# Start addresses of weight tiles, transposed activations and the SwiGLU product in a two-layer hybrid trunk

## The chip, the cores and the metric

The kernel runs on one core of a Trainium2 chip. The metric is the device time of one execution in microseconds (us). Before the change it is 2417.23 us, the median of three runs (2416.89 to 2418.15).

## What is computed

Two layers of a streaming-encoder trunk on one sequence of 256 rows by 2048 columns, in float32. Each layer projects the rows, runs three groups of heads, mixes them, and applies a SwiGLU feed-forward part; a layer norm follows each half.

```python
for li in range(DEPTH):                                   # DEPTH = 2
    proj = x @ w_in[li]                                   # 2048 -> 6920 columns
    qa, ka, va, qb, kb, vb, qc, kc, vc, oc, ic, fc = jnp.split(proj, SPLIT_POINTS, axis=-1)
    ya = diff_attention(qa, ka, va, lam[li], subln_a[li], li)
    yb = chunk_band_attention(qb, kb, vb, rel_bias[li])
    yc = mlstm(qc, kc, vc, oc, ic, fc, conv_w[li], norm_c[li])
    mix = jnp.concatenate([ya, yb, yc], axis=-1) @ w_out[li]          # 2048 -> 2048
    x = layer_norm(DEEPNORM_ALPHA * x + mix, ln1_g[li], ln1_b[li])
    ffn = (jax.nn.silu(x @ w_gate[li]) * (x @ w_up[li])) @ w_down[li] # 2048 -> 5632 -> 2048
    x = layer_norm(DEEPNORM_ALPHA * x + ffn, ln2_g[li], ln2_b[li])
```

## The kernel before

Almost all of the work is the products with the weights. `run_groups` works through them as a list of groups. In a layer there are seven input groups, `in.0` to `in.6` (`w_in`, 1024 columns each, the last 768), two groups for `w_out`, and then, for each half of the 5632 feed-forward columns, six groups for gate and up (1024, 1024 and 768 columns, first gate and then up: `ff.half.width.gate_or_up`) and two groups for `w_down` (`dn.half.block`). A group is a loop over `k`, steps of 128 rows of the weight (16 steps, in a `dn` group 22), and over `t`, the two halves of the sequence. Each float32 operand is held as two parts, a rounded one (`hi`) and the rest (`lo`), both of type float32r, and each product is made from three: `xh` by `whi`, `xh` by `wlo`, `xl` by `whi`. In TensorE's terms the piece of the transposed x (128 by 128) is the stationary operand, which a weight-load instruction brings into the array ahead of its matmul, and the weight row block (128 by 512, 384 or 256) is the moving one. A step of a group with two blocks is therefore six matmuls with six weight loads, all issued at L272:

```python
for i, (lt, wt) in enumerate(((xh, hi), (xh, lo), (xl, hi))):
    for b in bs:
        o, w = g["blocks"][b]
        nc.tensor.matmul(banks[t, b][:, 0:w], lt, wt[:, o:o + w], ...)
```

The order of the program is the order in which this Python code emits it; nothing is rescheduled. `convert` (L215) makes `whi` by a ScalarE cast (L224) and `wlo` by a VectorE subtraction (L225) from `raw`, which SyncE loads two steps at a time. `whi` and `wlo` have six buffers each, `raw` three. The stationary pieces come from two places. For the input, output, gate and up groups they lie in `xth` and `xtl`, made by `new_xt` (L288): a tile holds four `k` steps of 256 columns, there are four buffers ("slots") of each name, and a group goes through all four, four `k` steps in each. In the `dn` groups they lie in `gth` and `gtl` (L1031), one tile each that holds all 22 steps of the SwiGLU product. In the two names a piece is 512 bytes in each partition, and a piece starts a multiple of 512 bytes into its tile.

Between the products, `Tasks.tick` lets smaller tasks emit their instructions: attention heads, transposes, layer norm. `t_g` (L1085) transposes the SwiGLU product with 32x32 VectorE transposes (L408) and splits it into `gth` (ScalarE, L285) and `gtl` (VectorE, L286). The results of a group leave PSUM by ScalarE or VectorE (L428, L1037, L1041, L315); five PSUM banks serve the products, so a group's first matmul can wait for such an evacuation.

Of the kernel before, what the change touches and what calls it, by code (L numbers as in the profile page):

```python
# [10 lines left out]
F32 = mybir.dt.float32  # L11
F32R = mybir.dt.float32r
# [5 lines left out]
P = 128  # L18
SEQ = 256
# [14 lines left out]
KH = HALF_FF // P  # L34
# [11 lines left out]
FAR_AHEAD = 4  # L46
EVAC_ACT = (0, 1)
LAST_SKEW = 6
WARM = 9
MM_BUFS = 5  # L50
AUX_BUFS = 3
# [21 lines left out]


class Tasks:
    """Work that fills in between the weight products, a stage at a time.

    Units (attention heads) hold several buffers, so only a few of them run at once."""

    def __init__(self):  # L80
        self.q = []
# [46 lines left out]


def bcast(ap, n, offset, pattern):  # L130
    """A DRAM view read alike by n partitions."""
    return bass.AP(tensor=ap.tensor, offset=ap.offset + offset, ap=[[0, n]] + pattern)


class Trunk:
# [14 lines left out]
        self.flags = set()  # L150
        self.cms = {}

    # ---------------------------------------------------------------- set-up
    def setup(self):
        nc = self.nc
        c = self.const.tile([P, CONST_W], F32, name="cst_sb")
        self.cst_sb = c
        nc.scalar.dma_start(out=c[:, 0:P], in_=self.cst[:, 0:P])
        self.ident = c[:, 0:P]
        self.tri = c[:, P:2 * P]  # L160
        self.ones = c[:, 2 * P:3 * P]
        self.cmask = c[:, 3 * P:4 * P]
        o = 4 * P
        self.abias = c[:, o:o + A_HEADS * SEQ].rearrange("p (h k) -> p h k", h=A_HEADS)
        self.xs = [self.res.tile([P, D], F32, name=f"x{t}") for t in range(NT)]
        self.load_x(nc.sync, 0, 0)
        warm = self.const.tile([P, 512], BF16, name="warm")
        nc.vector.memset(warm, 0.0)
        wps = self.aux()
        for i in range(WARM):  # L170
            nc.tensor.matmul(wps, warm[:, 0:P], warm, start=True, stop=True)
        self.mhalf = self.const.tile([P, 2], F32, name="mhalf")
        nc.vector.memset(self.mhalf, -0.5)

    def load_x(self, eng, t, c):
# [20 lines left out]
    def aux(self):  # L196
        return self.psum.tile([P, 512], F32, name="aux", tag="aux", bufs=AUX_BUFS)

    # ------------------------------------------------------------- weight flow
    def load_pair(self, p):  # L200
        if p >= len(self.pairs):
            return
# [27 lines left out]
            self.load_pair(j // 2 + RAW_BUFS)  # L230

    def run_groups(self, groups):
        """Products x @ W over all groups; W streams through, split into two exact parts."""
        nc = self.nc
        self.steps, self.pairs, self.raws, self.whl = [], [], {}, {}
        for g in groups:
            g["base"] = len(self.steps)
            for k in range(g["nk"]):
                self.steps.append((g, k))
                if k % 2 == 0:  # L240
                    self.pairs.append(g["src"](k))
        for p in range(RAW_BUFS):
            self.load_pair(p)
            for c in {1: (1,), 2: (2, 3)}.get(p, ()):
                for t in range(NT):
                    self.load_x(nc.sync, t, c)
        done = 0
        for g in groups:
            nk, nb, si, so = g["nk"], len(g["blocks"]), g.get("skew_in", 1), g.get("skew_out", 1)
            allb = tuple(range(nb))  # L250
            order = [(k, t, allb) for t in range(NT) for k in range(si)]
            order += [(k, t, allb) for k in range(si, nk - so) for t in range(NT)]
            order += [(k, t, (b,)) for t in range(NT) for b in allb for k in range(nk - so, nk)]
            banks = {}
            g["start"]()
            for (k, t, bs) in order:
                j = g["base"] + k
                if (k, t, bs[-1]) == (nk - 1, NT - 1, nb - 1) and "mid" in g:
                    g["mid"]()
                xh, xl = g["lhs"](k, t)  # L260
                ahead = AHEAD if k >= nk - so or k < si else FAR_AHEAD
                while done < min(j + ahead + 1, len(self.steps)):
                    self.convert(done)
                    done += 1
                hi, lo = self.whl[j]
                for b in bs:
                    if (t, b) not in banks:
                        banks[t, b] = self.psum.tile([P, 512], F32, name="mm", tag="mm", bufs=MM_BUFS)
# [3 lines that stand above are left out]
                        nc.tensor.matmul(banks[t, b][:, 0:w], lt, wt[:, o:o + w],  # L272
                                         start=(k == 0 and i == 0), stop=(k == nk - 1 and i == 2))
                g["progress"] = k + 1
                if k == nk - 1:
                    for b in bs:
                        g["evac"](t, b, banks[t, b])
                if "after" in g and bs[-1] == nb - 1:
                    g["after"](k, t)
                if bs[-1] == nb - 1:  # L280
                    self.tasks.tick(g.get("budget", BUDGET) * g["width"] / 1024)

    # -------------------------------------------------------------- transposes
    def split(self, ps, hi, lo):
        self.nc.scalar.copy(out=hi, in_=ps)  # L285
        self.nc.vector.tensor_tensor(out=lo, in0=ps, in1=hi.bitcast(F32), op=ALU.subtract)  # L286

    def new_xt(self):  # L288
        return [self.xtp.tile([P, 4, SEQ], F32R, name=n, tag=n, bufs=4) for n in ("xth", "xtl")]

    def tr_block(self, srcs, dst, slot0, t):
        """Transpose [128 x 128] pieces into consecutive slots of a split block."""
        ps = self.aux()
        for i, s in enumerate(srcs):
            self.nc.tensor.transpose(out=ps[:, i * P:(i + 1) * P], in_=s, identity=self.ident)  # L295
        n = len(srcs)
        v = ps[:, 0:n * P].rearrange("p (k q) -> p k q", q=P)
        hi = dst[0][:, slot0:slot0 + n, t * P:(t + 1) * P]
        lo = dst[1][:, slot0:slot0 + n, t * P:(t + 1) * P]
        self.split(v, hi, lo)  # L300

    # ------------------------------------------------------------- layer norm
    def ln_load(self, g, b, l):
        nc = self.nc
        lg = self.lnpool.tile([P, D], F32, name="lng", tag="lng")
# [34 lines left out]
        nc.vector.scalar_tensor_tensor(out=z, in0=z, scalar=rs, in1=lb[:, s], op0=ALU.mult, op1=ALU.add)  # L340

    def xt_hooks(self, mvrs):
        """The transposed x by pieces: the first ones at once, the later ones while the products run."""
        xt = self.xt = [None] * 4
        applied, done = set(), set()
        piece = lambda k: next(i for i, (a, b) in enumerate(PIECES) if a <= k < b)
# [36 lines left out]
                    need(1, i)  # L383
        return dict(lhs=lhs, after=after, apply=apply, need=need)

    # ------------------------------------------------------------------ layer
    def attn_consts(self, l):
        nc, ap = self.nc, self.apool
        self.wg = self.const.tile([P, KD, 8], F32, name="wg", tag="wg")
# [12 lines left out]
        return self.apool.tile([P, 4, SEQ + 3], F32, name="qk", tag="qk", bufs=5)  # L402

    def dve_tr(self, out, in_, n):
        """Transpose n [128 x 128] tiles of in_ [P, n, 128] into out [P, n, 128] in four stages."""
        for i in range(4):
            for j in range(4):
                self.nc.vector.transpose(out=out[32 * j:32 * j + 32, 0:n, 32 * i:32 * i + 32],  # L408
                                         in_=in_[32 * i:32 * i + 32, 0:n, 32 * j:32 * j + 32])
            yield 1, 0.05 + 0.19 * n  # L410
# [7 lines left out]
        (self.nc.scalar.copy if t in EVAC_ACT else self.nc.vector.tensor_copy)(out=out, in_=in_)  # L418

    def evac_qk(self, t, bank, dst, scaled, scale, flag):  # L420
        """The first `scaled` of four tiles are queries and take the scale of the scores."""
        nc = self.nc
        stg = self.stg_tile()
        n = scaled * P
# [7 lines left out]
        while not all(f in self.flags for f in fl):  # L432
            yield 1, 0.0

    # -- C ---------------------------------------------------------------------
    def t_conv(self, l, blk):
        nc = self.nc
        yield from self.wait_flags("conv", (("cqk", blk), 0), (("cqk", blk), 1))
# [17 lines left out]
    def t_gates(self, l):  # L456
# [9 lines left out]
        for k in range(KD):  # L466
# [3 lines left out]
                                 stop=(k == KD - 1 and i == 2))  # L470
            if k % 8 == 7:
                yield 1, 0.0
        gT = ap.tile([8, SEQ], F32, name="gT")
        nc.scalar.copy(out=gT, in_=ps[0:8, 0:SEQ])
        yield 1, 0.3
        ps = self.aux()
# [111 lines left out]
        yield 1, 0.6  # L588

    def rms(self, ss, n, r):  # L590
        """r * (ss / n + eps) ** -0.5, all [P, k]."""
        nc = self.nc
        k = ss.shape[-1]
        ve = self.small.tile([P, 2], F32, name="rve")
# [29 lines left out]
            self.nc.gpsimd.tensor_tensor(out=y, in0=y, in1=self.nrm, op=ALU.mult)  # L624
        yield 1, 0.0

    # -- B ---------------------------------------------------------------------
    def t_bscore(self, h0, t):
        nc, ap = self.nc, self.bpool
        nb = t + 1  # L630
# [61 lines left out]
            self.flags.add(("B", h0, u))  # L692
        yield 1, 0.6

    # -- A ---------------------------------------------------------------------
    def t_aprep(self, l):
        nc, ap = self.nc, self.apool
        lam_init = 0.8 - 0.6 * math.exp(-0.3 * l)
# [72 lines left out]
        self.flags.add(("A", h, t))  # L771
        yield 1, 0.2

    # -- mix -------------------------------------------------------------------
    def mix_block(self, b):
        if self.mixt[b] is None:
            self.mixt[b] = self.new_xt()
        return self.mixt[b]

    def mix_ready(self, k, t):  # L780
        """Whether the k-th block of 128 columns of the mix (C, A, B) is in place."""
        return (("mix", k // 4, t) if k < 10 else ("B", (k - 10) // 2 * 2, t)) in self.flags

    def t_mix(self, b, t, last_in):
# [13 lines left out]
        self.flags.add(("mix", b, t))  # L798
        yield 1, 0.6

    # -- the groups of a layer ---------------------------------------------------
    def rows(self, w, l, r0, c0, width):
        return w[l, r0:r0 + 2 * P, c0:c0 + width].rearrange("(k p) n -> p k n", p=P)

# [209 lines left out]
    def ffn_groups(self, l):  # L1014
# [3 lines left out]
        for hf in range(2):  # L1018
            c = 0
            for wi, w in enumerate(widths):  # L1020
# [4 lines left out]
                for gu in range(2):  # L1025
# [2 lines left out]

                    def start(hf=hf, wi=wi, gu=gu):
                        if wi == 0 and gu == 0:  # L1030
                            self.gt = [self.gpool.tile([P, KH, SEQ], F32R, name=n, tag=n) for n in ("gth", "gtl")]  # L1031

                    def evac(t, b, bank, gu=gu, bw=bw, kt0=kt0, hf=hf):
                        nc = self.nc
# [96 lines left out]
```

## Time and profile before

| | before |
|---|---|
| median of 3 runs | 2417.23 us |
| profiled execution, span from first to last instruction | 2413.9 us |
| PE (TensorE matmul) busy | 2351.6 us, 97% of the span |
| PEld (weight loads, beside PE) busy | 1964.8 us, 81% |
| DVE (VectorE) busy | 1650.6 us, 68% |
| ACT (ScalarE) busy | 1029.1 us, 43% |
| matmuls of the weight products (L272) | 10176 of 10894 |
| mean granted TensorE clock | 0.990 |

The profile is of one execution. Its span leaves out 3.3 us of the median, which lie around the first and the last instruction. Matmuls are pipelined and their ends are modelled, so that one matmul's row overlaps the next: the duration of a row (some 390 ns for 512 columns) is not what a matmul costs. The cost is the time from one start to the next, which is the length of a stretch divided by the matmuls that the code issues in it. The count in a row of a stretch is one to two higher, since matmuls that began earlier are counted too.

### The profile page before, as it was taken

The numbers are of one execution on the slowest core, as the hardware profiler recorded it, in microseconds if no ns is written. First come the engines' busy times: TensorE is split into PE (matmuls) and PEld (weight loads), VectorE is DVE, ScalarE is ACT, GpSimd is POOL, SyncE is SP. The second block draws the span as 40 slices with busy tenths as digits, with TensorE's granted clock in tenths as the row PEclk, the third lists the DMA queues.
The fourth block names the chain that finished last, engine by engine and source line by source line (L and its number), as shares of the span: only waits on it lengthen the run. The fifth ranks groups of instructions, "written<-read, shape, count | busy, mean of one in ns | idle before, by whom it ended". The sixth has DMA issues, their size and how long they took to land.

```text
span 2413.9 us, 28566 instructions
## 1 busy us (share of the span) xinstructions
PE 2351.6 (97%) x10894; PEld 1964.8 (81%) x10894; DVE 1650.6 (68%) x2934; ACT 1029.1 (43%) x1355; POOL 58.1 (2%) x120
## 2 busy tenths in 40 slices
PE   9999999999999999999999999999999999999997
PEld 7787778888988888888787787788888888889886
DVE  5967786748666448667589576857577664486675
ACT  5444454444344344344344544544443443443442
POOL 0010010000000000000000101000000000000000
PEclk9999999999999999999999999999999999999999
DMA  8453546565556555565555544556555665555563
GB/s 293 164 187 122 177 155 194 191 217 193 156 184 209 192 192 188 160 193 192 175 192 172 177 144 153 167 199 209 192 192 144 199 210 188 196 190 156 184 209 105
DMA packets 126489, 441.19 MB, mean 183 GB/s; under 512 B 11824, under 2 KB 14864, under 8 KB 125328
## 3 DMA queue, kind: packets, MB, share of 16 engines
q1 hardware_dynamic: 126208, 439.31, 55.7%
q8 instruction: 85, 1.39, 0.2%
q14 instruction: 52, 0.43, 0.1%
q10 hardware_dynamic: 144, 0.07, 0.0%
HBM read 437.25 MB, written 2.10 MB: 182 GB/s over the span
## 4 chain that ended last, share of the span: by engine, by line
PE 81%; DVE 13%; ACT 2%; issue 2%; DMA 1%; POOL 1%; SPq 0%; POOLq 0%; ACTq 0%
PE mm L272 77%; DVE wlo L225 5%; DVE gtr L408 4%; DVE qk L408 2%; ACT whi L224 1%; PE aux L557 1%; PE aux L295 1%; DMA raw<-w_up 1%; PE aux L469 0%; DVE x L340 0%; DVE cacc L447 0%; DVE gtl L286 0%; DVE bst L319 0%; DVE cacc L450 0%; DMA x<-x 0%
## 5 line engine op out<-in xcount | busy, mean ns | idle before, releaser
L225 DVE TENSOR_TENSOR wlo<-raw,whi 128x1024 fp32r<-128x1024 f32 (+2 forms) x849 | 989.9, 1172 | 634.4 <-ACT whi L224 627.1
L224 ACT CAST whi<-raw 128x1024 fp32r<-128x1024 f32 (+2 forms) x849 | 847.4, 1009 | 994.2 <-PE mm L272 936.0
L272 PE MATMUL mm<-whi,xth 128*128 128x512 f32 (+2 forms) x2688 | 828.6, 383 | 31.5 <-ACT sil L1037 19.9
L272 PE MATMUL mm<-wlo,xth 128*128 128x512 f32 (+2 forms) x2688 | 817.2, 379 | 0.0
L272 PE MATMUL mm<-whi,xtl 128*128 128x512 f32 (+2 forms) x2688 | 814.8, 379 | 0.0
L272 PEld LDWEIGHTS mm<-whi,xth 128*128 128x128 f32 x2688 | 494.4, 189 | 119.8 <-ACT sil L1037 23.7
L272 PEld LDWEIGHTS mm<-whi,xtl 128*128 128x128 f32 x2688 | 500.9, 189 | 84.9 <-DVE xtl L286 0.6
L272 PEld LDWEIGHTS mm<-wlo,xth 128*128 128x128 f32 x2688 | 500.9, 189 | 84.5 <-issue 0.7
L408 DVE STREAM_TRANSPOSE gtr<-sil 32x128 f32<-32x128 f32 (+1 forms) x768 | 223.8, 291 | 11.3
L272 PE MATMUL mm<-whi,gth 128*128 128x512 f32 x704 | 226.1, 395 | 0.0
L272 PE MATMUL mm<-whi,gtl 128*128 128x512 f32 x704 | 226.1, 395 | 0.0
L272 PE MATMUL mm<-wlo,gth 128*128 128x512 f32 x704 | 226.0, 395 | 0.0
L408 DVE STREAM_TRANSPOSE qk<-stg 32x128 f32<-32x128 f32 x512 | 155.0, 303 | 8.8 <-ACT stg L426 0.4
L272 PEld LDWEIGHTS mm<-whi,gtl 128*128 128x128 f32 x704 | 132.5, 188 | 31.2
L272 PEld LDWEIGHTS mm<-wlo,gth 128*128 128x128 f32 x704 | 132.5, 188 | 31.2
L272 PEld LDWEIGHTS mm<-whi,gth 128*128 128x128 f32 x704 | 132.5, 188 | 30.8
L285 ACT CAST gth<-gtr 128x512 fp32r<-128x512 f32 (+1 forms) x48 | 28.1, 586 | 208.1 <-DVE gtr L408 208.1
L329 POOL TENSOR_SCALAR ve<-mv 128x1 f32<-128x1 f32 x8 | 4.7, 590 | 1740.0 <-DVE mv L327 1739.9
L285 ACT CAST xth<-aux 128x512 fp32r<-128x512 f32 (+1 forms) x58 | 29.3, 512 | 30.4 <-PE aux L295 25.0
L286 DVE TENSOR_TENSOR xtl<-aux,xth 128x512 fp32r<-128x512 f32 (+1 forms) x58 | 34.0, 594 | 5.0 <-ACT xth L285 4.7
L1041 DVE TENSOR_TENSOR sil<-mm,sil 128x512 f32<-128x512 f32 (+1 forms) x48 | 29.1, 643 | 11.8 <-PE mm L272 11.8
L452 ACT ACTIVATE qk<-cacc 128x256 f32<-128x256 f32 x24 | 10.0, 419 | 49.6 <-DVE cacc L450 49.6
(155 smaller groups left out, 716.4 us busy)
## 6 DMA issues: line engine op xcount, KB each, us to landing
raw<-w_in SPq DMA_DIRECT2D x94, 1024.0 KB, 4.9
raw<-w_down SPq DMA_DIRECT2D x88, 1024.0 KB, 5.2
raw<-w_gate SPq DMA_DIRECT2D x64, 1024.0 KB, 5.0
raw<-w_up SPq DMA_DIRECT2D x64, 1024.0 KB, 5.1
raw<-w_out SPq DMA_DIRECT2D x32, 1024.0 KB, 5.2
raw<-w_gate SPq DMA_DIRECT2D x32, 768.0 KB, 4.5
raw<-w_up SPq DMA_DIRECT2D x32, 768.0 KB, 4.4
raw<-w_in SPq DMA_DIRECT2D x16, 768.0 KB, 4.2
```

Source lines behind the costliest of these rows:

```text
L224: nc.scalar.copy(out=hi[:, s], in_=src[:, s])
L225: nc.vector.tensor_tensor(out=lo[:, s], in0=src[:, s], in1=hi[:, s].bitcast(F32), op=ALU.subtract)
L272: nc.tensor.matmul(banks[t, b][:, 0:w], lt, wt[:, o:o + w], start=(k == 0 and i == 0), stop=(k == nk - 1 and i == 2))
L285: self.nc.scalar.copy(out=hi, in_=ps)
L286: self.nc.vector.tensor_tensor(out=lo, in0=ps, in1=hi.bitcast(F32), op=ALU.subtract)
L295: self.nc.tensor.transpose(out=ps[:, i * P:(i + 1) * P], in_=s, identity=self.ident)
L329: nc.gpsimd.tensor_scalar(out=ve, in0=mv[:, 1:2], scalar1=1.0, scalar2=1e-5, op0=ALU.mult, op1=ALU.add)
L408: self.nc.vector.transpose(out=out[32 * j:32 * j + 32, 0:n, 32 * i:32 * i + 32], in_=in_[32 * i:32 * i + 32, 0:n, 32 * j:32 * j + 32])
L452: nc.scalar.activation(out=raw[:, i, 3:], in_=acc, func=AF.Silu)
L557: nc.tensor.matmul(ps[:, o:o + SEQ - q0], kt, qt, start=(i == 0), stop=(i == len(pieces) - 1))
L1041: nc.vector.tensor_tensor(out=g[:, 0:bw], in0=bank[:, 0:bw], in1=g[:, 0:bw], op=ALU.mult)
```

## The change

It changes where tiles lie in a partition, and no instruction of the products: on every engine the built programs have the same instructions in the same order with the same waits, but for one set-up memset, which writes 32 columns in place of 2.

- `mhalf` moves from the constants to the small tiles and grows to 32 columns. With it the tiles that follow the constants move down by 32 bytes, and `xth`, `raw`, `whi` and `wlo` begin at multiples of 512 bytes; the pool of `gth` begins at one too.
- `new_xt` makes tiles 128 bytes longer (`XT_PAD`, 32 elements). A tile's view is the same, so the four slots of `xth` begin 0, 128, 256 and 384 bytes past a multiple of 512, and so do the four of `xtl`.
- `gth` and `gtl` are 64 bytes longer (`GT_PAD`, 16 elements), so that `gtl` begins 64 bytes past a multiple of 512.
- `gT`, a tile of the gates, takes a buffer of `stg` to make room; blank lines take the place of docstrings and comments.

The starts in the built programs, in bytes past a multiple of 512 ("offset" is that of the stationary piece less that of the moving row, modulo 512):

| tile | start before | start after | offset before | offset after |
|---|---|---|---|---|
| `raw`, `whi`, `wlo` (moving) | 32 | 0 | | |
| `xth`, `xtl`, slot 0 / 1 / 2 / 3 | 32 / 32 / 32 / 32 | 0 / 128 / 256 / 384 | 0 | 0 / 128 / 256 / 384 |
| `gth` | 416 | 0 | 384 | 0 |
| `gtl` | 416 | 64 | 384 | 64 |
| `sil`, `gtr` | 416 | 128 | | |

The second block of a weight row begins 2048 bytes (in the 768-wide feed-forward groups 1536) after the first, again a multiple of 512.

```diff
+XT_PAD = 32
+GT_PAD = 16
...
-        self.mhalf = self.const.tile([P, 2], F32, name="mhalf")
+        self.mhalf = self.small.tile([P, 32], F32, name="mhalf", tag="mhalf", bufs=1)
...
     def new_xt(self):
-        return [self.xtp.tile([P, 4, SEQ], F32R, name=n, tag=n, bufs=4) for n in ("xth", "xtl")]
+        out = []
+        for n in ("xth", "xtl"):
+            x = self.xtp.tile([P, 4 * SEQ + XT_PAD], F32R, name=n, tag=n, bufs=4)
+            out.append(x[:, 0:4 * SEQ].rearrange("p (k q) -> p k q", q=SEQ))
+        return out
...
-        gT = ap.tile([8, SEQ], F32, name="gT")
+        gT = ap.tile([P, 512], F32, name="gT", tag="stg", bufs=3)[0:8, 0:SEQ]
...
-                            self.gt = [self.gpool.tile([P, KH, SEQ], F32R, name=n, tag=n) for n in ("gth", "gtl")]
+                            self.gt = []
+                            for n in ("gth", "gtl"):
+                                g = self.gpool.tile([P, KH * SEQ + GT_PAD], F32R, name=n, tag=n)
+                                self.gt.append(g[:, 0:KH * SEQ].rearrange("p (k q) -> p k q", q=SEQ))
```

## Rows read from the trace of the kernel before

**Rows 1.** The page: busy time of each engine; the ending chain's shares by line.

```profile
PE 2351.6 (97%) x10894; PEld 1964.8 (81%) x10894; DVE 1650.6 (68%) x2934; ACT 1029.1 (43%) x1355; POOL 58.1 (2%) x120
...
PE mm L272 77%; DVE wlo L225 5%; DVE gtr L408 4%; DVE qk L408 2%; ACT whi L224 1%; PE aux L557 1%; PE aux L295 1%; DMA raw<-w_up 1%; PE aux L469 0%; DVE x L340 0%; DVE cacc L447 0%; DVE gtl L286 0%; DVE bst L319 0%; DVE cacc L450 0%; DMA x<-x 0%
```

**Rows 2.** PE's groups by form: operation, count | busy us, mean ns | idle before.

```profile
L272 PE MATMUL mm<-whi,xth 128*128 128x512 f32 x2112 | 684.2, 396 | 12.1 <-ACT stg L428 11.0 <-ACT sil L1037 0.6
...
L272 PE MATMUL mm<-whi,gth 128*128 128x512 f32 x704 | 226.1, 395 | 0.0
L272 PE MATMUL mm<-whi,gtl 128*128 128x512 f32 x704 | 226.1, 395 | 0.0
...
L272 PE MATMUL mm<-whi,xth 128*128 128x384 f32 x512 | 136.4, 341 | 19.4 <-ACT sil L1037 19.4
...
L272 PE MATMUL mm<-whi,xth 128*128 128x256 f32 x64 | 17.8, 279 | 0.0
```

**Rows 3.** Stretches of one group each: length, busy us (instructions) by engine, PEclk, DMA.

```profile
55.10:98.62 43.52, 43.52 (x193) 36.04 (x192) 42.16 (x100) 17.46 (x22) 0.00 (x0) 1.00 0.49 158
548.40:591.92 43.52, 43.52 (x193) 36.05 (x192) 41.28 (x88) 18.29 (x21) 0.00 (x0) 1.00 0.53 173
875.40:918.92 43.52, 43.52 (x194) 36.05 (x193) 20.23 (x18) 17.46 (x18) 0.00 (x0) 1.00 0.59 194
2117.00:2160.52 43.52, 43.52 (x193) 36.05 (x192) 41.27 (x87) 17.95 (x20) 0.00 (x0) 1.00 0.51 171
635.80:669.11 33.31, 33.31 (x193) 33.27 (x193) 32.12 (x77) 12.77 (x17) 0.00 (x0) 1.00 0.49 147
...
709.10:770.44 61.34, 61.34 (x266) 49.77 (x265) 48.03 (x95) 24.17 (x26) 0.00 (x0) 1.00 0.59 195
770.50:831.84 61.34, 61.34 (x266) 49.72 (x265) 29.25 (x27) 23.09 (x22) 0.00 (x0) 1.00 0.58 189
...
2340.10:2401.50 61.40, 61.40 (x265) 49.34 (x263) 33.61 (x40) 17.82 (x17) 1.14 (x2) 1.00 0.38 123
```

**Rows 4.** PE in order of time in an up group: start us, us, operation, xcount.

```profile
559.76 0.61 PE L272 MATMUL mm<-wlo,xth 128*128 128x512 f32 x2
560.21 0.62 PE L272 MATMUL mm<-whi,xtl 128*128 128x512 f32 x2
560.66 0.62 PE L272 MATMUL mm<-whi,xth 128*128 128x512 f32 x2
561.12 0.61 PE L272 MATMUL mm<-wlo,xth 128*128 128x512 f32 x2
561.57 0.62 PE L272 MATMUL mm<-whi,xtl 128*128 128x512 f32 x2
```

**Rows 5.** The same view in a down group.

```profile
719.82 0.64 PE L272 MATMUL mm<-whi,gtl 128*128 128x512 f32 x2
720.29 0.62 PE L272 MATMUL mm<-whi,gth 128*128 128x512 f32 x2
720.75 0.62 PE L272 MATMUL mm<-wlo,gth 128*128 128x512 f32 x2
721.21 0.63 PE L272 MATMUL mm<-whi,gtl 128*128 128x512 f32 x2
721.68 0.64 PE L272 MATMUL mm<-whi,gth 128*128 128x512 f32 x2
```

**Rows 6.** All engines in order of time where a 768-wide up group begins.

```profile
669.15 0.34 PE L272 MATMUL mm<-whi,xth 128*128 128x384 f32 x1
...
671.81 0.62 ACT L285 CAST gth<-gtr 128x512 fp32r<-128x512 f32 x1 [6.01 <-DVE gtr L408]
...
673.80 1.62 ACT L1037 ACTIVATE sil<-mm 128x384 f32<-128x384 f32 x4
...
674.34 0.44 PE L272 MATMUL mm<-whi,xth 128*128 128x384 f32 x1 [4.85 <-ACT sil L1037]
```

**Rows 7.** Whom PE waited for in all: us, times, longest us.

```profile
PE mm L272 <- ACT sil L1037: 19.9, 6, 4.9
PE mm L272 <- ACT stg L428: 11.0, 2, 5.5
```

**Rows 8.** A stretch after that wait, columns as in rows 3.

```profile
674.80:677.60 2.80, 2.80 (x10) 2.80 (x10) 1.27 (x2) 1.34 (x3) 0.00 (x0) 0.50 0.96 302
```

**Rows 9.** PE in that stretch in order of time.

```profile
675.20 0.84 PE L272 MATMUL mm<-whi,xtl 128*128 128x384 f32 x2
675.84 0.84 PE L272 MATMUL mm<-whi,xth 128*128 128x384 f32 x2
676.48 0.84 PE L272 MATMUL mm<-wlo,xth 128*128 128x384 f32 x2
```

## The prediction

> **What bounds the kernel now.** The page comes first: PE is busy for 97% of the span, and of the chain that ended last 77% is one line, L272, the weight products [rows 1]. Next the forms of these products, for their counts: each row stands for one of the three products of a step, so there are 3 x 2112 = 6336 matmuls of 512 columns on `xth`/`xtl`, 3 x 512 = 1536 of 384 columns, 3 x 64 = 192 of 256, and 3 x 704 = 2112 of 512 on `gth`/`gtl`, with hardly any idle time before them [rows 2]. PE's time is thus their number times the time from one start to the next, and an address can matter only through that interval.
>
> The stretches give the interval. Four groups on `xth`/`xtl`, far apart and with VectorE busy for 20 or for 42 us beside them, all last 43.52 us for their 192 matmuls: 226.67 ns each [rows 3]. 512 columns at 2.4 GHz (PEclk 1.00) are 213.33 ns, so 13.3 ns are over. The 384-wide group gives 33.31 / 192 = 173.5 ns, 13.5 over its 160 [rows 3]. The down groups, with the same clock, the same 512 columns and the same order of products, need 61.34 us for 264 matmuls: 232.35 ns, 19.0 over, and the last of them 232.6 [rows 3]. In order of time, pairs of starts lie 0.45 or 0.46 us apart in the one kind of group, 0.46 or 0.47 in the other, with no idle time between [rows 4, 5]. The extra 5.68 ns cannot be VectorE's doing: one down group has 48 us of it, the next 29, and both last 61.34 [rows 3]. What differs is the offset between the stationary piece and the moving row: 0 for `xth`/`xtl`, 384 for `gth`/`gtl`. Pieces and rows lie many different multiples of 512 bytes apart and the 43.52 us do not change, so the offset counts modulo 512 or a divisor of it; 128 or less is excluded, since 384 would then be like 0.
>
> At half clock (PEclk 0.50) two 384-column matmuls take 0.64 us [rows 8, 9]: 320 ns each, exactly 384 columns at 1.2 GHz. What is over at full clock is therefore no fixed cost of the instruction; it looks like a stream that cannot be fed faster, disturbed more by some offsets of the weight load running beside it than by others.
>
> **The change, part by part.** No instruction, order or wait changes, so all terms are intervals.
>
> Slots of `xth`/`xtl`. A group passes through all four, a quarter of its matmuls in each: 2016 per slot of the 8064. Slot 0 keeps offset 0: no change. Slot 3 gets offset 384, which the down groups show: 2016 x 5.68 = 11.5 us. Offsets 128 and 256 have no row. The nearest rows are the two offsets that there are, 0 (nothing) and 384 (5.68 ns); below nothing cannot be excluded, since 13.3 ns are there to be won. I take 5.68 for both, since offset 0 looks like the special case: its intervals are one constant number, the down groups' vary. That is 23.0 us, with ends at 0 and 23. Together 34.4 us.
>
> What hides some of it. Where a 768-wide up group begins, PE waits 4.85 us: its PSUM bank is emptied by a ScalarE operation queued behind a cast that waited 6.01 us for VectorE's transposes [rows 6]. In the gate group ahead of it VectorE is busy for 32.12 of 33.31 us [rows 3], and its backlog, not PE, sets when the wait ends. A gate group that takes 144 x 5.68 ns = 0.8 us longer only shortens that wait. There are four such places (19.9 us in six waits), and two like them behind L428 (11.0 us in two) [rows 7]: 6 x 0.8 = 4.9 us hidden. Without that cover they are paid.
>
> `gth`/`gtl`. Four of a step's six matmuls use `gth`, which goes to offset 0: 1408 x 5.68 = 8.0 us if they fall to 226.67. `gtl` at 64 has no row; between 226.67 and 232.35 would be 0 to 4.0 us won, and I take none. But the offset now changes after every four and every two matmuls, and whether the constant interval is reached in so short a run no row shows. I take half of the 8.0, 4 us, with ends 0 and 12.
>
> `mhalf`, `gT` and the alignment of tiles for VectorE, ScalarE and the DMA: cost nothing. The bound is PE, and behind these tiles it waits 31 us in all [rows 7]; at worst these waits grow by a tenth, 3 us.
>
> Sum: 34.4 - 4.9 - 4 = 25.5 us, on the execution's span of 2413.9: 2439.4. The median lies 3.3 above the span, so **2442.7**, rounded to 2442.
>
> [...]
>
> **The rivals.**
>
> *Repeat at 256.* If the offset counts modulo 256, slot 2 is like slot 0, and two slots lose: 4032 x 5.68 = 22.9, less 6 x 0.55 hidden and 4 won: +15.6, 2433. The rows fit either period.
>
> *No net change.* Either the offset is not the cause, and nothing moves; or only 384 is bad, so that slot 3 loses 11.5 less 1.6 hidden, while the down groups win up to 12. Both give 2415 to 2417. For it: just one bad offset is seen. Against it: nothing else that tells the groups apart is seen.
>
> *Faster: the start itself.* Before, every moving row begins 32 bytes past a multiple of 512, now on one. If the 13.3 ns are the price of that start (a row that takes one more fetch than its bytes need), they go. For it: 512- and 384-column rows pay the same 13.3 to 13.5, and half clock pays nothing. Against it: down groups have the same start and pay more, so offset counts too. All of it would be 8064 x 13.3 + 2112 x 19.0 = 147 us. VectorE keeps some: four 768-wide gate groups cannot shorten (10 us), groups with 41.3 or 42.2 us of VectorE work can fall only to that (some 4 us), nor can the stretches behind L428 (5 us); that leaves 128 us, 2289. Half of the overhead gives about 2353. It decides from the point where the start saves more than the 4.3 ns (34.4 / 8064) that the slots lose. [...]
>
> **How the numbers follow.** All three offsets lose (forecast, 2442): 0.40. Repeat at 256 (2433): 0.19. No net change: 0.16. Faster by the start, or because 128 or 256 beats 0 (2289 to 2410): 0.20. Worse than the sum's upper end: 0.05. That end has no cover and no gain in the down groups, 2417 + 34.4 = 2452, with a little more for an offset worse than 384: 2456. The low end, 2405, takes in no change and small gains, and leaves out most of the fast case. A measurement of this kernel can tell 0.2% (4.8 us) from no change: faster 0.20, same 0.16, slower 0.64.
>
> **What would show it.** In the changed profile a 1024-wide gate or up group should last about 44.3 us, with stretches of 48 matmuls: 10.9 us in slot 0, 11.15 in the others. A slot's stretch of 10.9 proves its offset harmless. Down groups should fall to about 60.9 us; at 59.9 all the offset's cost is gone, at 61.34 none. The waits of 4.85 us should shrink to about 4. The prediction is wrong if a slot runs below 226.67 ns, above all slot 0, whose offset is unchanged and whose start is new.

## The result

The changed kernel takes 2434.59 us, the median of four runs (2429.96 to 2437.50), beside 2417.06 us for the kernel before in the same comparison (2415.01 to 2418.15). The ratio is 1.0072, with a 95% interval of 1.0058 to 1.0087: it is slower by 0.7%. A second series of five runs (below, "the spread of the runs") gave 2431.11 us, a ratio of 1.0057 (1.0044 to 1.0071). The forecast was 2442.7, the rival *repeat at 256* said 2433.

The profiled execution has a span of 2431.5 us, 17.6 us more than before. Its page has the same engines with the same work; PE became busier, by 22 us, and the weight loads beside it (PEld) by 8.6 us (compare [rows 1]). Columns: busy us, share of the span, instructions.

```profile
PE 2373.6 (98%) x10894; PEld 1973.4 (81%) x10894; DVE 1650.7 (68%) x2934; ACT 1028.6 (42%) x1355; POOL 58.1 (2%) x120
```

The main reading is a 1024-wide gate group taken apart by slot. In [rows 3] this group lasts 43.52 us (548.40:591.92), 10.88 us for each 48 of its matmuls. The same view of the changed kernel (PE alone: stretch, length, busy us and count, PEclk, DMA share and GB/s) has one row per slot, in the order in which the group goes through them: offsets 0, 384, 256, 128. The next four rows are the 768-wide gate group, in the same order of offsets, and the last two are down groups, with `gth` at offset 0 and `gtl` at 64.

```profile
556.06:566.95 10.89, 10.89 (x49) 1.00 0.41 142
566.95:578.11 11.16, 11.16 (x50) 1.00 0.51 162
578.11:589.00 10.89, 10.89 (x50) 1.00 0.44 139
589.00:600.16 11.16, 11.16 (x50) 1.00 0.74 259
644.25:652.60 8.35, 8.35 (x50) 1.00 0.18 30
652.60:661.04 8.44, 8.44 (x49) 1.00 0.55 175
661.04:669.37 8.33, 8.33 (x50) 1.00 0.61 187
669.37:677.81 8.44, 8.44 (x49) 1.00 0.61 186
717.50:778.51 61.01, 61.01 (x266) 1.00 0.59 196
778.50:839.51 61.01, 61.01 (x265) 1.00 0.59 190
```

Slots at 0 and 256 take 10.89 us for 48 matmuls, 226.9 ns each; slots at 128 and 384 take 11.16, 232.5 ns. At 512 columns that is the whole answer on the slots: 256 costs nothing, 128 costs what 384 costs. In the 768-wide group the bad slots lose much less: its four rows last 33.56 us together, beside 33.31 before [rows 3], which is 0.25 us on 96 matmuls in the two bad slots, 2.6 ns each. The down groups fall from 61.34 to 61.01 us.

The waits of PE shrink a little, 19.9 to 18.2 us and 11.0 to 9.7 us, and the longest from 4.9 to 4.5 and from 5.5 to 4.8 (compare [rows 7]; whom PE waited for: us, times, longest).

```profile
PE mm L274 <- ACT sil L1046: 18.2, 4, 4.5
PE mm L274 <- ACT stg L434: 9.7, 2, 4.8
```

One place does not fit any interval. The input group 3 of layer 0 lasts 65.0 us before (149.60:214.60 at PEclk 1.00) and 68.48 us after, at a mean clock of 0.95; for 6.8 us of it the granted clock is 0.50, half of full speed. The rows are the group and the stretch in it; then the same group before, with all engines ahead of PEclk.

```profile
150.66:219.14 68.48, 68.48 (x311) 0.95 0.39 132
187.30:194.10 6.80, 6.80 (x16) 0.50 0.10 10
```

```profile
149.60:214.60 65.00, 65.00 (x311) 49.52 (x310) 35.62 (x89) 32.77 (x57) 9.41 (x17) 1.00 0.42 140
```

In time order, the clock is low from the attention scores of a head on (float32 matmuls on `qk`). Eight matmuls take 3.65 us, 2.05 us before. Start us, us, operation, count; first the changed kernel, then the kernel before.

```profile
187.33 3.65 PE L563 MATMUL aux<-qk 128*128 128x256 f32 x8
```

```profile
186.01 2.05 PE L557 MATMUL aux<-qk 128*128 128x256 f32 x8
```

Ahead of that, PE had been busy without a break since the group began (as far as the modelled ends tell), at full clock. The row is that stretch of the changed kernel, with all engines (PE, PEld, DVE, ACT, POOL) ahead of PEclk.

```profile
150.70:187.20 36.50, 36.50 (x187) 28.32 (x186) 19.96 (x49) 20.37 (x30) 6.12 (x8) 1.00 0.47 160
```

The same happens in layer 1: first the changed kernel, then the kernel before.

```profile
1355.93:1424.42 68.49, 68.49 (x311) 0.95 0.40 133
```

```profile
1347.47:1412.54 65.07, 65.07 (x311) 1.00 0.42 140
```

The two groups are 6.9 us longer than before together, and the next section shows that some 0.8 us of that belong to the slots.

### The profile page after: what moved, and what is told of

It reads as the page before. It is cut to its first block, busy times and chain, and to the rows that moved or that the text cites. A ratio compares the mean times of both kernels' runs of the same rounds, so it can differ in the third digit from the quotient of the medians.

```text
span 2431.5 us, 28566 instructions
## 1 busy us (share of the span) xinstructions
PE 2373.6 (98%) x10894; PEld 1973.4 (81%) x10894; DVE 1650.7 (68%) x2934; ACT 1028.6 (42%) x1355; POOL 58.1 (2%) x120
## 4 chain that ended last, share of the span: by engine, by line
PE 81%; DVE 13%; issue 2%; ACT 2%; DMA 1%; POOL 1%; SPq 0%; POOLq 0%; ACTq 0%
PE mm L274 78%; DVE wlo L227 4%; DVE qk L414 3%; DVE gtr L414 3%; ACT whi L226 1%; PE aux L563 1%; PE aux L301 1%; PE aux L475 0%; DMA raw<-w_out 0%; DVE cacc L453 0%; DVE x L346 0%; DVE sil L1050 0%; DVE bst L325 0%; PE aux L734 0%; DMA raw<-w_in 0%
## 5 line engine op out<-in xcount | busy, mean ns | idle before, releaser
L274 PE MATMUL mm<-whi,xth 128*128 128x512 f32 (+2 forms) x2688 | 836.5, 386 | 28.3 <-ACT sil L1046 18.2
L274 PEld LDWEIGHTS mm<-whi,xth 128*128 128x128 f32 x2688 | 495.8, 190 | 119.7 <-ACT sil L1046 19.9
```

Source lines behind the costliest of these rows:

```text
L274: nc.tensor.matmul(banks[t, b][:, 0:w], lt, wt[:, o:o + w], start=(k == 0 and i == 0), stop=(k == nk - 1 and i == 2))
```

## Experiments

Unless said otherwise, the diffs are against the changed kernel. `self.gap(pool, name, n)` is a tile of n float32 columns that nothing uses: it leaves 4n bytes free. Four of the experiments have a single run; its total also holds the clock's drops, so these are read by their stretches, all at PEclk 1.00.

**Everything at offset 0.**

```diff
-XT_PAD = 32
-GT_PAD = 16
+XT_PAD = 0
+GT_PAD = 0
```

> The change with both paddings taken out: weight rows, all four slots of xth and xtl, and gth and gtl begin at multiples of 512, so every offset is 0. Offset theory (the interval follows the offset between piece and moving row, modulo 256): every 1024-wide group 43.52 us (226.67 ns each), down groups 59.9 us in place of 61.34, so 2417 - 8 x 1.45 = 2405 us. Theory of the start (it matters that rows begin at 512): groups on xth and xtl would also fall below 43.52 us. Theory that the down groups are slow for another reason than offset: down groups stay at 61 us, 2417 us.

Measured: 2404.05 us (five runs, 2402.04 to 2406.25), ratio to before 0.995 (0.9937 to 0.9962). The rows are the gate group and the two first down groups.

```profile
548.79:592.31 43.52, 43.52 (x193) 1.00 0.51 173
709.89:769.77 59.88, 59.88 (x265) 1.00 0.60 200
769.77:829.61 59.84, 59.84 (x265) 1.00 0.60 194
```

59.88 us for 264 matmuls are 226.8 ns. The down groups were slow by their offset, which explains all but 0.1 ns of the difference, and moving the row's start from 32 to 0 past a multiple of 512 gave nothing (43.52 before and here). The rival *faster: the start itself* falls. This kernel beats both.

**The same from the other side: only `gth` and `gtl` moved.** Against the kernel before: 128 bytes are left free ahead of `gth`, so that it begins at 32, as the weight rows do there.

```diff
+                            self.gap(self.gpool, "gt", 32)
                             self.gt = [self.gpool.tile([P, KH, SEQ], F32R, name=n, tag=n) for n in ("gth", "gtl")]
```

> The kernel before with nothing changed but gth and gtl, moved up by 128 bytes, so that they begin 32 past a multiple of 512, as the weight rows do there: offset 0 everywhere, no tile aligned to 512. Offset theory: the same as with everything at 512: down groups 59.9 us, 2405 us. Theory that alignment to 512 is needed: down groups stay above that, 2410 us or more.

Measured: 2403.64 us (2402.46 to 2405.02), ratio 0.9949 (0.9935 to 0.9962), the same time as with everything at 0.

```profile
548.30:591.82 43.52, 43.52 (x194) 1.00 0.51 174
709.06:768.94 59.88, 59.88 (x266) 1.00 0.60 200
```

Neither the pieces nor the rows begin at a multiple of 512 here. The offset matters, the alignment does not. One free stretch of 128 bytes would have been the change to make.

**Weight rows moved under fixed slots.**

```diff
+        self.gap(self.wp, "w", 32)
         raw = self.wp.tile([P, 2, 1024], F32, name="raw", tag="raw", bufs=RAW_BUFS)
```

> The changed kernel with raw, whi and wlo (and the pool of gth and gtl) moved up by 128 bytes; slots of xth and xtl stay at 0, 128, 256, 384. Offset theory: the slots change places, 128 and 384 run at 226.7 ns, 0 and 256 at 232.4 ns; the group time stays 44.1 us and the whole 2434 us. Theory of the piece's own start: the slots at 0 and 256 stay the fast ones. Theory of the moving row's start: all slots change alike.

Measured: 2430.56 us (four runs, 2430.09 to 2435.61), ratio 1.0063 (1.0050 to 1.0077). The gate group by slot, in order the slots that begin at 0, 384, 256 and 128, whose offsets are now 384, 256, 128 and 0.

```profile
552.55:563.70 11.15, 11.15 (x49) 1.00 0.41 147
563.70:574.60 10.90, 10.90 (x50) 1.00 0.50 162
574.60:585.75 11.15, 11.15 (x49) 1.00 0.44 135
585.75:596.64 10.89, 10.89 (x49) 1.00 0.73 267
```

The slots that begin at 0 and 256 (offsets 384 and 128 here) are now the slow ones, those that begin at 384 and 128 (offsets 256 and 0) the fast ones. It is the distance between piece and row that counts, not where either lies.

**Only the slots.** `gth` and `gtl` go back to offset 384.

```diff
-GT_PAD = 16
+GT_PAD = 0
...
+                            self.gap(self.gpool, "gt", 96)
                             self.gt = []
```

> The changed kernel with gth and gtl put back to offset 384; only the slots of xth and xtl differ from before. Offset theory: groups on xth and xtl as in the changed kernel (44.1 us), down groups 61.34 us as before, so 8 x 0.33 = 2.6 us above the changed kernel, 2437 us. If the down groups' gain had been the slots' doing, they would stay at 61.0 us.

Measured: 2430.21 us (four runs, 2428.82 to 2434.34), ratio 1.0060 (1.0046 to 1.0074). The rows are input group 3, the gate group and a down group.

```profile
150.20:215.63 65.43, 65.43 (x311) 1.00 0.40 138
552.27:596.37 44.10, 44.10 (x194) 1.00 0.53 177
713.73:775.08 61.35, 61.35 (x265) 1.00 0.59 196
```

The parts behave as expected (44.10, 61.35), but the total does not lie 2.6 us above the changed kernel, it lies 4 below. The first row says why: input group 3 takes 65.43 us at PEclk 1.00. Up to this point nothing differs from the changed kernel, which spent 68.48 us here. So 0.4 us of the group's loss are the slots, and 3.05 us the clock.

**Smaller offsets, and 0 against 256 in the down groups.** The slots lie 32 bytes apart, and a gap puts `xtl` on the same offsets as `xth`.

```diff
-XT_PAD = 32
-GT_PAD = 16
+XT_PAD = 8
+GT_PAD = 64
...
         for n in ("xth", "xtl"):
+            self.gap(self.xtp, n, {"xth": 0, "xtl": 96}[n])
...
+        self.gap(self.xtp, "end", 96)
         return out
```

> The changed kernel with the slots of xth and xtl at offsets 0, 32, 64 and 96, and gth and gtl at 0 and 256. Theory that only 0 (modulo 256) is free and every other offset costs what 128 costs: slots of 32, 64 and 96 at 232.4 ns, 1024-wide groups 44.3 us. Theory that the cost grows with the distance from 0 up to 128: 228, 229.5, 231 ns, groups about 43.9 us. In the down groups 0 and 256 alternate: if only the remainder by 256 counts, 226.7 ns and 59.9 us as with both at 0; if a change of address between pieces breaks the constant interval, 61 us as with 0 and 64.

Measured: 2432.99 us (one run). By slot: offsets 0, 96, 64, 32; then a down group.

```profile
555.34:566.24 10.90, 10.90 (x49) 1.00 0.40 141
566.24:577.48 11.24, 11.24 (x49) 1.00 0.51 165
577.48:588.68 11.20, 11.20 (x49) 1.00 0.43 130
588.68:599.88 11.20, 11.20 (x49) 1.00 0.75 276
718.64:778.52 59.88, 59.88 (x265) 1.00 0.60 199
```

Against the 10.88 us of 48 matmuls before, 32, 64 and 96 cost 0.32 to 0.36 us, more than 128 does (0.28); there is no slope. At 384 columns the same offsets cost little: the 768-wide gate group lasts 33.39 us, 0.08 us more than before (33.31 [rows 3]).

```profile
644.42:677.81 33.39, 33.39 (x193) 1.00 0.49 145
```

The down group, with 0 and 256 in turn, is as fast as with 0 alone.

**The other half of the circle, and 64 by itself.** Slots at 128, 160, 192 and 224; `gth` and `gtl` both at 64. Against the kernel of the last experiment:

```diff
-GT_PAD = 64
+GT_PAD = 0
...
-            self.gap(self.xtp, n, {"xth": 0, "xtl": 96}[n])
+            self.gap(self.xtp, n, {"xth": 32, "xtl": 96}[n])
...
-        self.gap(self.xtp, "end", 96)
+        self.gap(self.xtp, "end", 64)
...
+                            self.gap(self.gpool, "gt", 16)
                             self.gt = []
```

> The changed kernel with the slots of xth and xtl at offsets 128, 160, 192 and 224, and gth and gtl both at 64. Theory that every offset but 0 costs the same: all four slots at 232.4 ns, groups 44.6 us. Theory of distance: 232.4, 231, 229.5, 228 ns, the mirror of 128, 96, 64, 32. Down groups: they show what 64 costs without a change between gth and gtl; 61.3 us if 64 costs as much as 384, 59.9 us if it is free and the 61.0 us of the changed kernel came from the change between 0 and 64.

Measured: 2447.30 us (one run). By slot: offsets 128, 224, 192, 160; then a down group.

```profile
557.29:568.45 11.16, 11.16 (x49) 1.00 0.40 141
568.45:579.65 11.20, 11.20 (x50) 1.00 0.51 171
579.65:590.64 10.99, 10.99 (x49) 1.00 0.42 130
590.64:601.85 11.21, 11.21 (x50) 1.00 0.76 272
719.86:781.46 61.60, 61.60 (x265) 1.00 0.58 195
```

192 is the mildest, 229.0 ns; 64 alone costs 61.60 us in a down group (233.3 ns), a little more than 384. It is no mirror: 64 costs 0.32 us in 48 matmuls, 192 only 0.11. Neither theory of the expectation holds exactly; "all but 0 cost about the same" is nearer, with 192 as the exception.

**Two offsets within a step.** `xth` at 0 and `xtl` at 128, `gth` at 0 and `gtl` at 128.

```diff
-XT_PAD = 32
-GT_PAD = 16
+XT_PAD = 0
+GT_PAD = 32
...
         for n in ("xth", "xtl"):
+            self.gap(self.xtp, n, {"xth": 0, "xtl": 32}[n])
...
+        self.gap(self.xtp, "end", 224)
         return out
```

> The changed kernel with all slots of xth at offset 0 and all of xtl at 128, and gth and gtl at 0 and 128, so that four of a step's six matmuls have a free offset and two do not. Theory that each weight load's own offset decides: a third of the matmuls at 232.4 ns, the mean 228.6, groups 43.9 us, down groups 60.4 us. Theory that the constant interval needs several matmuls of offset 0 in a row to come back: the mean near 231 to 232 ns, groups 44.4 us, down groups 61 us.

Measured: 2452.50 us (one run), the slowest of all. Gate group and down group:

```profile
563.91:608.54 44.63, 44.63 (x194) 1.00 0.52 179
727.63:788.99 61.36, 61.36 (x266) 1.00 0.58 196
```

With four of six pieces at the free offset, the group is longer (232.4 ns a matmul) than with half of its slots at a bad one (44.10): a mix within a step costs as much as a bad offset alone, so a matmul's interval does not follow from the offset of one piece alone. The second theory gives the right time, but its reason is not shown. In the changed kernel slot 256 comes right after slot 384 and lasts 10.89 us, 0.01 above 48 matmuls of the low interval; there the low interval is back after one or two matmuls. Why runs of four do not bring it back stays open. The changed kernel's down groups, with 0 and 64 mixed in the same way, fit: 61.01 us, nearer to the 61.60 of 64 alone than to 59.88.

**Offsets that are no multiple of 32.** Slots at 16, 48, 80 and 112, since the view begins 16 bytes into a tile; `gth` and `gtl` at 0. Against the kernel with slots at 0, 32, 64 and 96:

```diff
-GT_PAD = 64
+GT_PAD = 0
...
-            out.append(x[:, 0:4 * SEQ].rearrange("p (k q) -> p k q", q=SEQ))
+            out.append(x[:, 4:4 + 4 * SEQ].rearrange("p (k q) -> p k q", q=SEQ))
```

> The changed kernel with the slots of xth and xtl at offsets 16, 48, 80 and 112, and gth and gtl both at 0. Theory that every offset but 0 costs the same: all four slots 232.4 ns. Theory of distance: 227.4, 228.8, 230.2, 231.7 ns. An interval below 226.67 ns in any slot would say that 0 is not the best offset. Down groups 59.9 us.

Measured: 2434.00 us (one run). By slot: offsets 16, 112, 80, 48; then a down group.

```profile
556.46:567.67 11.21, 11.21 (x50) 1.00 0.41 141
567.67:578.86 11.19, 11.19 (x49) 1.00 0.52 172
578.86:590.00 11.14, 11.14 (x49) 1.00 0.42 132
590.00:601.20 11.20, 11.20 (x50) 1.00 0.76 274
719.53:779.41 59.88, 59.88 (x265) 1.00 0.60 199
```

Sixteen bytes off is already as bad as any in this group. Of the twelve offsets tried from 0 to 224, none is faster than 0.

**The spread of the runs.** The changed kernel as it is, and the changed kernel with `gth` and `gtl` both at 0.

```diff
-GT_PAD = 16
+GT_PAD = 0
```

> The changed kernel once more, as it is, for the spread of its runs. Its profile holds stretches of half clock in input group 3 of both layers that the profile of before and that of the slots-only kernel do not hold, though up to there the slots-only kernel has the same instructions at the same addresses in xth, xtl, whi and wlo. Theory that these drops come by chance from run to run: times between about 2428 (clock 0.990) and 2437 us (clock 0.985), the lower the clock the longer. Theory that they belong to the changed kernel: all runs at 2433 us or more with the clock at 0.986.

Measured: 2431.11 us (2428.53 to 2431.87). The shortest run has a mean granted clock of 0.989, the others 0.986 to 0.988. The first series had 2429.96 us at 0.988, 2433.29 and 2435.89 at 0.986, 2437.50 at 0.985. One kernel, nine runs from 2428.5 to 2437.5 us, longer as the clock is lower, with one exception (2430.99 us at 0.986). The profiled execution shows that the drops come and go: in input group 3 the clock stays at 1.00 in layer 0 (65.43 us, as in the slots-only kernel) and drops in layer 1. The rows are the two groups.

```profile
151.23:216.66 65.43, 65.43 (x311) 1.00 0.41 139
1353.82:1422.30 68.48, 68.48 (x312) 0.95 0.40 132
```

The 2433 us or more that the other theory wanted of every run did not come.

> The changed kernel with gtl at offset 0 in place of 64, so that gth and gtl are both at 0 and only the slots of xth and xtl lose. Offset theory: down groups 59.9 us in place of 61.01, 8 x 1.13 = 9 us below the changed kernel, 2425 us; still slower than before, by 8 us. If the down groups' gain does not add to the slots' loss, the time stays above 2428 us.

Measured: 2422.82 us (11 runs, 2418.58 to 2424.46), ratio 1.0020 (1.0011 to 1.0029). Its runs lie in two bunches, 2418.6 to 2419.4 us at clock 0.990 and 2422.8 to 2424.5 at 0.987 or 0.988, with two between. The median is 8 us below the changed kernel's second series; 9 were expected. A down group shows the gain by itself:

```profile
719.31:779.16 59.85, 59.85 (x266) 1.00 0.61 199
```

Gain and loss add.

## Why the prediction was right, and where not

The direction, the mechanism (the interval follows the offset) and the range (2405 to 2456) held; the likeliest case did not. Point by point:

- *PE's interval is what an address can change.* Right: VectorE's and ScalarE's busy time moved by 0.5 us at most, PE's by 22.
- *The offset between piece and row counts.* Right, and shown by moving the rows under fixed slots.
- *Slot 3 at 384 loses 5.68 ns a matmul.* Right for 512 columns: 11.16 us for 48, 232.5 ns. Wrong for the 384-column matmuls, where a bad slot loses 2.6 ns ((33.56 - 33.31) / 96); I had carried the price from 512 to 384 columns without a row. Two slots of 384 columns come to 2 x 384 x 2.6 ns = 2.0 us, where the price of 512 columns gives 4.4.
- *I take 5.68 for both 128 and 256.* This is the step that failed. 128 was right, 256 costs nothing: 2016 matmuls that I had charged 11.5 us. The rows fitted a period of 256 as well as one of 512, the rival said so and gave 2433; I preferred the longer period because offset 0 "looked like the special case", which it is, but of every 256 bytes.
- *4.9 us hidden behind waits.* The direction was right: the waits of 30.9 us fell to 27.9, 3 us. With half of the slots slow, 3.3 had been the rival's figure. 
- *Down groups gain 4 us.* Measured 8 x 0.33 = 2.6 us. The doubt behind the halving was right: a mix of free and costly pieces does not earn the free ones' share, and 64 costs by itself.
- *The start of the row.* I gave the fast case 0.20. It is gone: rows at 32 and at 0 cost 226.67 ns alike.
- *The clock* was no term of the sum. Of the 17.6 us in the profiled execution, (68.48 - 65.43) us in input group 3 of each layer, 6.1 us, are drops of the granted clock that the slots-only kernel did not have at the same place. Without them its span would be 2425.4, some 4 us below what *repeat at 256* gave for the span (2413.9 + 15.6). So its nearness to the measured time is part luck: its intervals overstate the loss, and the clock, of which it said nothing, made up for it. The slots-only kernel, whose mean clock is that of before (0.990), has a span of 2428.8 us, 14.9 more than before, where this rival's terms for the slots give 22.9 - 3.3 = 19.6. The 384-column price is 2.4 us of the difference; the rest was not taken apart.

The rival *no net change* (2415 to 2417) falls with the time, 2434.59 us, and with the slots: a matmul's interval changes from 226.9 to 232.5 ns with nothing but the distance between the moving row and the piece loaded beside it, and 128 loses as 384 does. Where the loss arises no run shows.

What stays open: why. The runs show that the interval depends on the offset, that 0 and 256 give 226.7 ns and 128 and 384 give 232.5, each pair alike, that all other offsets tried give more than 226.7 too, and that a mix within a step costs as much as a bad offset. Nor is it shown what the remaining 13.3 ns are; no offset brought a whole slot or group below 226.67. They are an estimate themselves: groups of 512 and of 384 columns, 226.67 and 173.5 ns a matmul [rows 3], lie 53.2 ns apart, 0.416 ns a column, which is 2.4 columns per ns at PEclk 1.00, and the 320 ns of 384 columns at PEclk 0.50 [rows 8, 9] are 1.2 per ns; 512 columns at 2.4 per ns are 213.3 ns. The stream that cannot be fed faster, in the prediction, is a guess that no run tested. Whether it is the weight load of the next matmul or of the same one was not separated. Nor do the runs show why the clock drops came more often with the changed slots. Six of the twelve traces have one in input group 3 of a layer (the changed kernel twice, weight rows moved, 128 to 224, two offsets within a step, `gth` and `gtl` both at 0; mean clocks 0.986 to 0.988), and the other six, that of before and that of the slots-only kernel among them, have none there (0.988 to 0.990). In the times: the 15 runs of before in the last comparison lie within 2.8 us (2415.60 to 2418.38), while ten of the 28 runs of kernels with slots at 0, 128, 256 and 384 lie 4 us or more above the lowest run of their series.

## What to carry to other kernels

When equal matmuls differ in their start-to-start interval between two places of a kernel, compare the start addresses of their operands modulo a few powers of two before looking at the schedule. Here a distance of 0 or 256 bytes (modulo 512) between stationary piece and moving row is free, and every other one that was tried costs 1 to 3.3% of a matmul of 512 columns; one free stretch of 128 bytes ahead of `gth` makes the kernel before 0.5% faster (2403.64 us). Where two known values fit two periods, forecast the two apart, and carry a price measured at one width to another only with a row.

## What the runs showed of the hardware

- Float32r matmuls of 512 columns start every 226.67 ns at best over a whole group at PEclk 1.00 (43.52 us for 192), by the estimate above 13.3 ns more than their columns, whatever the start of the moving row (0 or 32 past a multiple of 512). Offsets of 16 to 224 bytes between row and piece gave 229.0 to 234.2 ns over 48 matmuls, 0 and 256 gave 226.9.
- The price depends on the width: offsets 128 and 384 cost 2.6 ns at 384 columns and 5.6 ns at 512. Offsets 32, 64 and 96 cost 6.7 to 7.5 ns at 512 columns and at 384 less than 1 ns (0.08 us on 144 matmuls).
- The granted clock fell to 0.50 for 6.8 us at a place where PE was busy throughout, from float32 matmuls of the attention scores on (eight of them took 3.65 us, 2.05 at PEclk 1.00), in some runs and not in others, at about 3 us each (68.48 us for the group beside 65.43).
